# Experts' first rows and second rows gathered in separate phases, the second rows token by token and summed over partitions by TensorE, with five dense passes instead of four

## The chip, the cores and the metric

The kernel runs on one core of one Trainium2 chip. The metric is the device time of one execution in microseconds (us); lower is better. TensorE is called PE here, VectorE DVE, ScalarE ACT, GpSimd POOL and SyncE SP, as in the profile.

## The reference

Two layers over 512 tokens of 1,024 features, in float32. Each layer mixes tokens (attention and a recurrence), normalises, and then lets each token use 128 of 16,384 "experts", each of which is one row `u` and one row `v`:

```python
# one layer, cut to what matters
m = x @ w_in                                   # q, k, v, recurrent branch, gates
y = sigmoid(ga) * (DiffAttention(m) @ w_br_attn) + sigmoid(gr) * (RGLRU(m) @ w_br_lru)
x = layer_norm(ALPHA * x + y @ w_out)
# experts: 8 heads choose 16 rows each from the scores of two sets of 128 keys
e, g = choose(x @ peer_wq, subkeys)            # (token, 128) indices and weights
act = gelu(einsum('cd,ced->ce', x, u[e]))      # dot of the token with its 128 u rows
ffn = einsum('ce,ced->cd', g * act, v[e])      # weighted sum of its 128 v rows
x = layer_norm(ALPHA * x + ffn)
```

## The kernel before, in words

Tokens are cut into four blocks of 128, one token per partition. A *dense pass* (`mixer`, `route`, `route_late`) takes a pair of blocks of one layer from the projections to the choice of experts. It reads 96 chunks of weights, 512 KB each, through SP's DMA queue; `proj_T` and `proj_N` multiply them. There are four passes. The first one, with which nothing else can run, uses split operands (`Acts`): each float32 value is the sum of two float32r parts, and each product is made of three float32r products. The others use plain float32.

The *experts* (`experts`) of a block are 128 gathers, one per chosen expert rank j. A gather is one indirect DMA from POOL (line 730): for each of the 128 tokens, the 8 KB row of its j-th expert, `u` and `v` side by side, 1 MB in all. DVE multiplies the first half of the tile by the tokens and sums it (line 733: the dot); for every two gathers three small DVE operations and two small ACT operations turn the dots into weights; then the second half is added to the result either by DVE (line 703, into `acc`) or by PE (line 709), which multiplies it by a diagonal matrix that ACT makes out of the weights (line 707) and accumulates over the gathers in PSUM (`pv`). There are 1,024 gathers and 8 gather buffers.

The order of the work is written by `run`: gathers are a stream, and each dense pass is spread over a span of gathers by the table `PLAN`; a scheduler then fixes the order on each engine. A block's gathers begin when its first experts are chosen, so nothing is gathered until the first pass is nearly through.

Of the kernel before, what the change touches and what calls it, by code (L numbers as in the profile page):

```python
# [52 lines left out]
PLAN = (  # L53
# [4 lines left out]
)  # L58
V_ALONE = 0.5
MAXN = P * max(len(p[1]) for p in PLAN)  # L60
C_CHUNK = 1.75  # weight of 8 products of [128, 128] by [128, 128] in the issue order
HGS = {True: (1, 1, 2, 2, 2), False: (2, 2, 2, 2)}  # heads whose experts are chosen together


def weave(a, b, pace=1.0):
# [12 lines left out]
class Acts:  # L78
# [3 lines left out]
    def __init__(self, plain=None, hi=None, lo=None):  # L82
        self.plain = plain
        self.hi, self.lo = hi, lo
        self.split = plain is None


class Decoder:
    def __init__(self, ctx, tc, x, wpk, gpk, spk, cpk, lnv, lqk, uv, out):
        self.tc, self.nc = tc, tc.nc  # L90
        self.x, self.wpk, self.gpk, self.spk = x, wpk, gpk, spk
        self.cpk, self.lnv, self.lqk, self.uv, self.out = cpk, lnv, lqk, uv, out
# [6 lines left out]
        self.gp = pool("gather", 8)  # L99
        self.pp = pool("peer", 2)  # L100
        PS = dict(space=bass.MemoryType.PSUM)
        self.ps_mm = pool("ps_mm", 2, **PS)
        self.ps_s = pool("ps_s", 1, **PS)
        self.ps_t = pool("ps_t", 1, **PS)
        self.ps_v = pool("ps_v", 1, **PS)

    # ---------------------------------------------------------------- set-up
    def setup(self):
# [3 lines left out]
        # base bias: B[p, m] = (m - 384) - p where that is <= 0, else a large negative  # L112
# [10 lines left out]
        self.lnrows = cp.tile([16, 512], F32, name="lnrows")  # L123
        self.junk_a = cp.tile([P, P], BF16, name="junk_a")
# [3 lines left out]
        # tokens in two halves; the second's room serves the first dense part before  # L128
# [4 lines left out]
        self.e = [cp.tile([P, P], I32, name=f"e{b}") for b in range(NB)]  # L133
        self.g = [cp.tile([P, P], F32, name=f"g{b}") for b in range(NB)]
# [8 lines left out]
    def room(self, tag, dtype=F32, pool=None):  # L143
        """[128, 8, 256] for activations, in one of a few places."""
# [3 lines left out]
    def layer_consts(self, l):  # L148
# [18 lines left out]
        # softplus(-lambda) = log1p(exp(-|lambda|)) + max(-lambda, 0)  # L167
# [26 lines left out]
    # ---------------------------------------------------------------- helpers  # L194
# [5 lines left out]
    def split_weight(self, hi, lo, l, ch):  # L200
        """A chunk's weights in float32r parts whose sum they are."""
        raw = self.wp.tile([P, D], F32, name="raw", tag="w")
        self.nc.sync.dma_start(raw, self.wpk[l, ch])
        self.nc.scalar.copy(hi, raw)  # L204
        self.nc.vector.tensor_tensor(lo, raw, hi.bitcast(F32), ALU.subtract)  # L205

    def proj_T(self, l, ch, act, n, ps=None):
        """[chunk columns, tokens] of (tokens) @ w."""
        if ps is None:
            ps = self.ps_mm.tile([P, 512], F32, name="ps_mm", tag="mm")  # L210
        if act.split:
            t = self.gp.tile([P, 2, D], F32R, name="wsp", tag="uv")
            self.split_weight(t[:, 0], t[:, 1], l, ch)
            hi, lo = (t[:, i].rearrange("p (k c) -> p k c", k=KC) for i in range(2))
            passes = ((hi, act.hi), (hi, act.lo), (lo, act.hi))
        else:
            passes = ((self.weight(l, ch), act.plain),)
        steps = [(w[:, kc, :], x[:, kc, :n]) for w, x in passes for kc in range(KC)]
        for i, (w, x) in enumerate(steps):
            self.nc.tensor.matmul(ps[:, :n], w, x, start=i == 0, stop=i == len(steps) - 1)  # L220
        return ps

    def proj_N(self, l, ch, act, blocks):
# [458 lines left out]
    def experts(self, l, b, G=2):  # L682
# [60 lines left out]
        for _ in prev:  # L743
            pass
# [92 lines left out]
```

## Time and profile before

| | |
|---|---|
| time, median of 3 runs (lowest to highest) | 3567.16 us (3563.05 to 3572.27) |
| profiled execution, span | 3564.2 us |
| busy: PE, DVE, ACT, POOL | 83%, 81%, 30%, 35% |
| moved by DMA | 1290.77 MB, 362 GB/s over the span |

The span is the time from the first to the last instruction of the one execution that was profiled; no other time of that execution is shown. It lies 3 us under the median of the timed runs and within their range, so a sum made against the span can be read as a time of the runs, give or take those 3 us. The shares are averages over stages with different limits.

### The profile page before, as it was taken

Reading aid. Unit: us, or ns where it says so; the run is one execution under the profiler, and the core shown is the slowest. Engines: PE = TensorE matmul, PEld = TensorE weight load, DVE = VectorE, ACT = ScalarE, POOL = GpSimd, SP = SyncE. Lnnn points to the kernel's source line nnn. Section 1 sums busy time; section 2 is a strip of 40 time slices with the busy share of each in tenths; the row PEclk is TensorE's granted clock in tenths of the full one; section 3 lists DMA queues with packets and bytes.
Section 4 is the critical chain, followed back from the end, with each engine's and each line's share of the span. In section 5 each row is a group of like instructions: output and inputs, shape, how many; then the busy total and the mean of one; then the engine's idle time right before and its main releaser. Section 6 shows DMA issues by size and latency. Waiting matters only on the chain.

```text
span 3564.2 us, 41600 instructions
## 1 busy us (share of the span) xinstructions
PE 2963.9 (83%) x11804; PEld 1907.9 (54%) x11804; DVE 2883.3 (81%) x9658; ACT 1085.1 (30%) x3174; POOL 1264.4 (35%) x1033
## 2 busy tenths in 40 slices
PE   8996878999999689999998689999898676655555
PEld 7995635677756346777654256677755222211111
DVE  7765799998768987777778977798778977788887
ACT  7842213442122234421222134432122121112111
POOL 0001234344332333333332443333333344456553
PEclk9997999999999889999999799999999889877777
DMA  6454889999999899999999899999999899999997
GB/s 200 159 167 178 299 326 384 390 411 416 418 385 366 341 362 403 390 375 387 395 396 365 296 409 395 371 409 418 418 382 349 298 394 421 421 421 407 422 421 318
DMA packets 219141, 1290.77 MB, mean 362 GB/s; under 512 B 24592, under 2 KB 37136, under 8 KB 87840
## 3 DMA queue, kind: packets, MB, share of 16 engines
q0 software_dynamic: 147456, 1073.81, 75.1%
q1 hardware_dynamic: 71456, 214.30, 16.1%
q8 instruction: 96, 1.57, 0.2%
q14 instruction: 133, 1.09, 0.1%
HBM read 1285.92 MB, written 2.10 MB: 361 GB/s over the span
## 4 chain that ended last, share of the span: by engine, by line
PE 35%; DVE 29%; DMA 20%; issue 8%; POOL 4%; ACT 4%; POOLq 0%; SPq 0%; DVEq 0%; ACTq 0%
DMA uvt<-uv_dram,e 20%; PE ps_mm L220 14%; PE pv L709 12%; DVE uvt L733 10%; DVE junk_d L660 5%; PE ps_mm L242 4%; POOL uvt L730 4%; DVE acc L703 3%; DVE si L627 1%; DVE sv L625 1%; PE ps_ln L297 1%; PE s L348 1%; PE pg L451 1%; PE ps_qk L220 1%; DVE ca L645 1%
## 5 line engine op out<-in xcount | busy, mean ns | idle before, releaser
L730 POOL DMA_INDIRECT uvt<-uv_dram,e x1024 | 1261.8, 1232 | 2268.7 <-DVE acc L703 598.8
L709 PE MATMUL pv<-uvt,dg 128*128 128x512 f32 x2588 | 1394.3, 680 | 483.3 <-ACT dg L707 481.9
L733 DVE SCALAR_TENSOR_TENSOR uvt<-uvt,xn 128x1024 f32<-128x1024 f32 x1024 | 1243.9, 1220 | 180.6 <-DMA uvt<-uv_dram,e 179.5
L709 PEld LDWEIGHTS pv<-uvt,dg 128*128 128x128 f32 x2588 | 521.0, 213 | 1206.7 <-ACT dg L707 703.2
L220 PE MATMUL ps_mm<-room_xT,w 128*128 128x256 f32 x3072 | 717.2, 382 | 3.4 <-ACT room_xT L252 2.9
L220 PEld LDWEIGHTS ps_mm<-room_xT,w 128*128 128x128 f32 x3072 | 576.5, 191 | 140.3 <-issue 58.6
L738 ACT ACTIVATE q<-dots 128x2 f32<-128x2 f32 x512 | 103.7, 203 | 1284.0 <-DVE uvt L733 1234.7
L703 DVE SCALAR_TENSOR_TENSOR acc<-uvt,w,acc 128x1024 f32<-128x1024 f32 x377 | 483.2, 1282 | 8.1
L707 ACT ACTIVATE dg<-ident,w 128x128 f32<-128x128 f32 x647 | 241.9, 397 | 184.7 <-DVE w L696 117.5
L660 DVE SCALAR_TENSOR_TENSOR junk_d<-iota,pf,ca 128x54 bf16<-128x54 f32 x1024 | 215.9, 268 | 0.4
L693 ACT ACTIVATE q<-q 128x2 f32<-128x2 f32 x512 | 103.7, 202 | 212.9 <-DVE q L691 204.3
L691 DVE SCALAR_TENSOR_TENSOR q<-q,dots 128x2 f32<-128x2 f32 x512 | 81.3, 159 | 103.2 <-ACT q L738 72.6
L696 DVE SCALAR_TENSOR_TENSOR w<-q,w 128x2 f32<-128x2 f32 x512 | 80.5, 157 | 88.0 <-ACT q L693 86.4
L205 DVE TENSOR_TENSOR wsp<-raw,wsp 128x1024 fp32r<-128x1024 f32 x96 | 116.2, 1221 | 18.3 <-ACT wsp L204 18.0
L220 PE MATMUL ps_mm<-room_xT,wsp 128*128 128x256 f32 x768 | 114.9, 292 | 0.5 <-ACT wsp L204 0.5
L204 ACT CAST wsp<-raw 128x1024 fp32r<-128x1024 f32 x96 | 98.7, 1047 | 20.1 <-issue 6.0
L220 PEld LDWEIGHTS ps_mm<-room_xT,wsp 128*128 128x128 f32 x768 | 102.0, 196 | 4.7 <-issue 2.4
L242 PE MATMUL ps_mm<-w,room_m 128*128 128x128 f32 x768 | 92.1, 282 | 6.9 <-DVE room_m L508 6.9
L242 PEld LDWEIGHTS ps_mm<-w,room_m 128*128 128x128 f32 x768 | 91.3, 198 | 12.0 <-DVE room_m L508 7.5
L242 PEld LDWEIGHTS ps_mm<-w,room_xT 128*128 128x128 f32 x768 | 92.6, 195 | 9.4 <-issue 7.7
L625 DVE MAX8 sv<-sc 128x8 f32<-128x128 f32 x128 | 36.5, 289 | 73.2 <-ACT sc L590 64.6
L242 PE MATMUL ps_mm<-w,room_xT 128*128 128x128 f32 x768 | 94.6, 278 | 0.0
(193 smaller groups left out, 3030.9 us busy)
## 6 DMA issues: line engine op xcount, KB each, us to landing
w<-wpk_dram SPq DMA_DIRECT2D x288, 512.0 KB
raw<-wpk_dram SPq DMA_DIRECT2D x96, 512.0 KB
uvt<-uv_dram,e POOLq DMA_INDIRECT x1024
gw<-gpk_dram SPq DMA_DIRECT2D x32, 128.0 KB
sk<-spk_dram SPq DMA_DIRECT2D x64, 64.0 KB
xn<-x_dram SPq DMA_DIRECT2D x4, 512.0 KB
out_dram<-xn SPq DMA_DIRECT2D x8, 256.0 KB
lq<-lqk_dram SPq DMA_DIRECT2D x2, 128.0 KB
```

The lines of the kernel that those rows point to most:

```text
L204: self.nc.scalar.copy(hi, raw)
L205: self.nc.vector.tensor_tensor(lo, raw, hi.bitcast(F32), ALU.subtract)
L220: self.nc.tensor.matmul(ps[:, :n], w, x, start=i == 0, stop=i == len(steps) - 1)
L242: self.nc.tensor.matmul(out[:, i], x(slice(i * P, (i + 1) * P)), w, start=j == 0, stop=j == len(steps) - 1)
L660: nc.vector.scalar_tensor_tensor(out=self.junk_d[:, k % 4, :NCAND], in0=self.iota, scalar=pf[:, h, k : k + 1], in1=ca[:, 1, h], op0=ALU.is ...
L693: nc.scalar.activation(q, q, AF.Tanh, scale=C_GELU)
L703: nc.vector.scalar_tensor_tensor(out=acc, in0=t[:, D:], scalar=w[:, i : i + 1], in1=acc, op0=ALU.mult, op1=ALU.add)
L707: nc.scalar.activation(dg, self.ident, AF.Copy, scale=w[:, i : i + 1])
L709: nc.tensor.matmul(pv[:, half], dg, t[:, D + half * 512 : D + (half + 1) * 512], start=not used[1], stop=j == P - 2)
L730: nc.gpsimd.indirect_dma_start(out=t, out_offset=None, in_=self.uv, in_offset=bass.IndirectOffsetOnAxis(ap=e[:, j : j + 1], axis=0))
L733: nc.vector.scalar_tensor_tensor(out=t[:, :D], in0=t[:, :D], scalar=1.0, in1=x, op0=ALU.mult, op1=ALU.mult, accum_out=dots[:, i : i + 1])
L738: nc.scalar.activation(q, dots, AF.Square, scale=A_GELU)
```

## The change

The table of rows is cut in two, `u` and `v`. A block's experts become two phases. `phase_u` gathers the 128 first rows per rank as before (line 625), but only their 4 KB; the dots read the tokens from a copy in PSUM (`xps`). When all 128 are there, the weights are made for the whole block at once and transposed by PE. `phase_v` gathers the second rows by token: one gather takes the 128 rows of one token, one per partition, with the transposed indices `eT`. PE then sums over the partitions: the weights of the token are the one non-zero column of a strip of 32 columns (`ring`), and four tokens that lie in different quarters of the partitions write four strips of 32 partitions of `pv` (line 681). DVE adds no more rows, ACT makes no more diagonals. There are 2,048 gathers of 512 KB and 13 gather buffers of half the size.

`STREAM` is the order of the phases: u of the first block; u of the second beside v of the first, alternately; v of the second; and so on for each pair. The dense passes are five: blocks 0 and 1 of the first layer have one each, with products of 128 columns, and all passes use plain float32. PSUM is now four banks used by turns for all dense work (`bank`), two for `xps` and two for `pv`.

```diff
+STREAM = [s for l in range(2) for h in (0, 2) for s in (
+    (("u", l, h),), (("u", l, h + 1), ("v", l, h)), (("v", l, h + 1),))]
 PLAN = (
-    (0, [0, 1], 0, 0, 32, 64, (0.5, 0.0, 0.0)),
-    (0, [2, 3], 60, 205, 245, 360, (0.7, 0.0, 0.25)),
-    (1, [0, 1], 258, 430, 485, 600, (0.7, 0.0, 0.25)),
-    (1, [2, 3], 516, 690, 740, 860, (0.7, 0.0, 0.25)),
+    (0, [0], 0, 0, 70, 70),
+    (0, [1], 6, 104, 126, 126),
+    (0, [2, 3], 130, 385, 500, 636),
+    (1, [0, 1], 516, 860, 1010, 1148),
+    (1, [2, 3], 1028, 1400, 1520, 1660),
 )
...
-        self.gp = pool("gather", 8)
+        self.gp = pool("gather", 13)
...
-        self.ps_mm = pool("ps_mm", 2, **PS)
-        self.ps_s = pool("ps_s", 1, **PS)
-        self.ps_t = pool("ps_t", 1, **PS)
+        self.ps_mm = pool("ps_mm", 4, **PS)
+        self.ps_x = pool("ps_x", 1, **PS)
         self.ps_v = pool("ps_v", 1, **PS)
...
+        if h0 + HG == H:
+            ps = self.bank("ps_e")
+            nc.tensor.transpose(ps[:, :P], self.eF, self.ident)
+            nc.vector.tensor_copy(self.eT[b], ps[:, :P])
...
+    def phase_u(self, l, b):
...
+        for j in range(P):
...
+            if j == 0:
+                x = self.ps_x.tile([P, D], F32, name="xps", tag="xps")
+                nc.scalar.copy(x, self.xn[b])
+            t = self.row(self.u, self.e[b][:, j : j + 1])
+            nc.vector.scalar_tensor_tensor(out=t, in0=t, scalar=1.0, in1=x, op0=ALU.mult,
+                                           op1=ALU.mult, accum_out=dots[:, j : j + 1])
...
+        ps = self.bank("ps_w")
+        nc.tensor.transpose(ps[:, :P], dots, self.ident)
...
+    def phase_v(self, l, b):
...
+        for r in range(32):
...
+            for g in range(4):
+                t = 32 * g + r
+                ts.append(self.row(self.v, self.eT[b][:, t : t + 1]))
...
+            for half in range(2):
+                for g in range(4):
+                    o = 32 * (8 * g + k) + 31 - r
+                    nc.tensor.matmul(pv[32 * g : 32 * g + 32, half], ring[:, o : o + 32],
+                                     ts[g][:, half * 512 : (half + 1) * 512], start=r == 0,
+                                     stop=r == 31)
```

Three places of the engines' orders. First POOL, whose rows are the gathers (`e_108` to `e_111` are the indices of blocks 0 to 3; of the change `e_106`, `e_107` those of blocks 0 and 1, and `eT_110` the transposed ones of block 0), behind the last constant. Before:

```order
L121 IOTA iota 128x54
L730 DMA uvt<-uv_dram,e_108 128x2048 x128
L730 DMA uvt<-uv_dram,e_109 128x2048 x128
L730 DMA uvt<-uv_dram,e_110 128x2048 x128
L730 DMA uvt<-uv_dram,e_111 128x2048 x128
```

And of the change:

```order
L625 DMA row<-u_dram,e_106 128x1024 x128
L625 DMA row<-u_dram,e_107 128x1024
L625 DMA row<-v_dram,eT_110 128x1024
L625 DMA row<-u_dram,e_107 128x1024
L625 DMA row<-v_dram,eT_110 128x1024
```

No second row is gathered before the first gather of block 1's first rows is issued. Next DVE in the change, from dot 128, the last of block 0 (line 641 is the dot; lines 305 to 310 are the softmax of block 1's attention, 387 to 436 its recurrence, 646 and 649 make the weights of block 0):

```order
L641 SCALAR_TENSOR_TENSOR row,dots<-row,xps 128x1024
L305 SCALAR_TENSOR_TENSOR pr<-base,ps_s 128x256 x2
L428 SCALAR_TENSOR_TENSOR thx<-thx,xc 128x128
L309 TENSOR_REDUCE at_st<-pr 128x2
L422 SCALAR_TENSOR_TENSOR mu<-mu,tl 128x128
L310 TENSOR_SCALAR at_st<-at_st 128x2
L387 COPY xr<-hist 128x3
L646 SCALAR_TENSOR_TENSOR q<-q,dots 128x128
L649 TENSOR_TENSOR dots<-dots,g_118 128x128
L430 SCALAR_TENSOR_TENSOR mu<-thx,mu 128x128
```

In this place 386 DVE instructions, the rest of block 1's dense pass with its output projection (line 488) and its layer norm and a part of its choice of experts, stand before dot 129, and no dot among them. Last PE, in the middle of a dense pass. Before (line 709 adds second rows, 128 columns of weights by 512; the others are dense products):

```order
L242 MATMUL ps_mm<-w,room_xT 128x128 x16
L348 MATMUL s_11621<-kT_104,qT 128x128 x2
L709 MATMUL pv<-uvt,dg 128x512 x4
L374 MATMUL pt<-ident,pr 128x128 x2
L220 MATMUL ps_mm<-room_xT,w 128x256 x2
```

And of the change, where the second rows of block 0 begin (line 681; the first size is the 32 partitions of the strip):

```order
L653 MATMUL ps_w<-ident,dots 128x128
L230 MATMUL ps_xt<-ident,xn_4987 128x128 x8
L681 MATMUL pv<-row,ring_114 32x512
L209 MATMUL ps_mm<-room_xT,w 128x256 x16
L681 MATMUL pv<-row,ring_114 32x512 x7
L209 MATMUL ps_mm<-room_xT,w 128x256 x8
L402 MATMUL pg<-xc,gw 128x256 x2
```

Sums of second rows now come eight at a time (four tokens by two halves) and wait for the four gathers of their tokens.

## Rows read from the trace of the kernel before

**Rows 1.** Page, parts 1 and 2: span, engines, DMA in 40 slices.

```profile
span 3564.2 us, 41600 instructions
...
PE 2963.9 (83%) x11804; PEld 1907.9 (54%) x11804; DVE 2883.3 (81%) x9658; ACT 1085.1 (30%) x3174; POOL 1264.4 (35%) x1033
...
DMA  6454889999999899999999899999999899999997
GB/s 200 159 167 178 299 326 384 390 411 416 418 385 366 341 362 403 390 375 387 395 396 365 296 409 395 371 409 418 418 382 349 298 394 421 421 421 407 422 421 318
```

**Rows 2.** Page, part 3: DMA queues; packets, MB, share of 16 engines.

```profile
q0 software_dynamic: 147456, 1073.81, 75.1%
q1 hardware_dynamic: 71456, 214.30, 16.1%
```

**Rows 3.** Windows: length, then PE, PEld, DVE, ACT, POOL, PEclk, DMA share, GB/s.

```profile
0.00:319.00 319.00, 287.64 (x2208) 271.93 (x2208) 213.26 (x545) 196.95 (x386) 2.57 (x9) 0.97 0.48 156
319.00:550.00 231.00, 171.92 (x673) 103.93 (x674) 198.44 (x1186) 57.84 (x185) 69.69 (x62) 0.91 0.86 322
...
1000.00:1300.00 300.00, 248.21 (x755) 140.59 (x754) 257.71 (x1403) 75.91 (x255) 98.95 (x88) 0.90 0.90 357
1300.00:1800.00 500.00, 479.72 (x2069) 343.93 (x2068) 368.99 (x901) 164.90 (x502) 176.73 (x146) 0.96 0.98 391
...
1900.00:2100.00 200.00, 143.95 (x319) 65.40 (x318) 178.07 (x935) 43.19 (x145) 79.51 (x64) 0.85 0.90 342
...
2700.00:2900.00 200.00, 142.59 (x334) 66.16 (x333) 179.07 (x1001) 38.38 (x144) 70.12 (x64) 0.88 0.88 328
2900.00:3530.00 630.00, 381.87 (x590) 128.42 (x589) 502.35 (x999) 116.35 (x405) 331.88 (x251) 0.80 1.01 419
```

**Rows 4.** DMA from 3250 to 3500 us: gathers of 8 KB rows alone.

```profile
DMA packets 14461, 105.36 MB, mean 421 GB/s; under 512 B 1602, under 2 KB 1602, under 8 KB 1602
```

**Rows 5.** DMA from 9 to 14 us: weights in rows of 4 KB alone.

```profile
DMA packets 607, 2.03 MB, mean 406 GB/s; under 512 B 70, under 2 KB 126, under 8 KB 607
```

**Rows 6.** Groups of DVE by form: line, count, busy us, mean ns, idle.

```profile
L733 DVE SCALAR_TENSOR_TENSOR uvt<-uvt,xn 128x1024 f32<-128x1024 f32 x1024 | 1243.9, 1220 | 180.6 <-DMA uvt<-uv_dram,e 179.5 <-issue 0.3
L703 DVE SCALAR_TENSOR_TENSOR acc<-uvt,w,acc 128x1024 f32<-128x1024 f32 x377 | 483.2, 1282 | 8.1
L660 DVE SCALAR_TENSOR_TENSOR junk_d<-iota,pf,ca 128x54 bf16<-128x54 f32 x1024 | 215.9, 268 | 0.4
...
L746 DVE SCALAR_TENSOR_TENSOR xn<-acc,pv 128x1024 f32<-128x1024 f32 x8 | 9.8, 1220 | 3.7 <-PE pv L709 3.4
```

**Rows 7.** Line 730, POOL's gathers: shortest, median, longest ns; first and last start.

```profile
L730 POOL DMA_INDIRECT uvt<-uv_dram,e x1024: 935/942/3133, 319.9 to 3532.5; - x171
```

**Rows 8.** Timeline of POOL near the end: start, length, line, idle before.

```profile
3253.83 1.94 POOL L730 DMA_INDIRECT uvt<-uv_dram,e  x1 [0.30 <-issue]
...
3274.20 0.94 POOL L730 DMA_INDIRECT uvt<-uv_dram,e  x1 [0.30 <-issue]
3275.44 0.94 POOL L730 DMA_INDIRECT uvt<-uv_dram,e  x1 [0.30 <-issue]
```

**Rows 9.** Timeline of DVE at the same place, two dots in a row.

```profile
3254.87 1.22 DVE L733 SCALAR_TENSOR_TENSOR uvt<-uvt,xn 128x1024 f32<-128x1024 f32 x1
...
3256.01 1.22 DVE L733 SCALAR_TENSOR_TENSOR uvt<-uvt,xn 128x1024 f32<-128x1024 f32 x1
```

**Rows 10.** Timeline of PE in the second pass.

```profile
813.49 1.88 PE L709 MATMUL pv<-uvt,dg 128*128 128x512 f32 x4
815.30 1.14 PE L348 MATMUL s<-kT,qT 64*128 64x256 f32 x8
...
828.43 3.72 PE L220 MATMUL ps_mm<-room_yr,w 128*128 128x256 f32 x16
```

**Rows 11.** Groups of PE by form: dense products of 128 columns.

```profile
L242 PE MATMUL ps_mm<-w,room_m 128*128 128x128 f32 x768 | 92.1, 282 | 6.9 <-DVE room_m L508 6.9
```

More of the change, by code (lines that the diff above doesn't have):

```diff
@@ L133, in setup @@
         self.e = [cp.tile([P, P], I32, name=f"e{b}") for b in range(NB)]
+        self.eT = [cp.tile([P, P], I32, name=f"eT{b}") for b in range(NB)]
+        self.w = {}
+        self.ring = [cp.tile([P, 32 * (RING + 1)], F32, name=f"ring{i}") for i in range(2)]
+        for r in self.ring:
+            nc.gpsimd.memset(r, 0.0)
         self.g = [cp.tile([P, P], F32, name=f"g{b}") for b in range(NB)]
@@ L198, in weight @@
         return w
[L200 to L220, printed above, removed]
-        return ps
@@ L264, in transpose_x, with bank, proj_T, proj_N @@
-    def transpose_x(self, act, i, b):
+    def bank(self, name):
+        return self.ps_mm.tile([P, 512], F32, name=name, tag="mm")
+    def proj_T(self, l, ch, x, n):
+        ps = self.bank("ps_mm")
+        w = self.weight(l, ch)
+        for kc in range(KC):
+            self.nc.tensor.matmul(ps[:, :n], w[:, kc, :], x[:, kc, :n], start=kc == 0,
+                                  stop=kc == KC - 1)
+        return ps
+    def proj_N(self, l, ch, x, blocks):
+        ps = self.bank("ps_mm")
+        w = self.weight(l, ch)
+        out = ps.rearrange("p (b c) -> p b c", c=P)
+        for i in range(len(blocks)):
+            for kc in range(KC):
+                self.nc.tensor.matmul(out[:, i], x[:, kc, i * P : (i + 1) * P], w[:, kc, :],
+                                      start=kc == 0, stop=kc == KC - 1)
+        return out[:, : len(blocks)]
@@ L271, in transpose_x, with layer_norm @@
                                     self.xn[b][:, kc * P : (kc + 1) * P], self.ident)
-            self.keep(act, (slice(None), slice(half * 4, half * 4 + 4), slice(i * P, (i + 1) * P)),
-                      ps.rearrange("p (k t) -> p k t", k=4))
-    def layer_norm(self, l, which, rows, eps, junk):
+            nc.scalar.copy(x[:, half * 4 : half * 4 + 4, i * P : (i + 1) * P],
+                           ps.rearrange("p (k t) -> p k t", k=4))
+    def layer_norm(self, l, which, rows, eps):
         nc, t2 = self.nc, self.t2
@@ L322, in project @@
         def project(h):
[L324 to L325 removed]
+            pk = self.proj_T(l, CH_K + h, x, n)
             k0 = t0 % (2 * P)
@@ new lines, in phase_v @@
+    def phase_v(self, l, b):
+        nc, pp = self.nc, self.pp
+        yield ("weights", l, b)
+        pv = self.ps_v.tile([P, 2, 512], F32, name="pv", tag="pv")
+        w = self.w[l, b].rearrange("p (g r) -> p g r", g=4)
+        x = self.xn[b]
+        for r in range(32):
+            ring, k = self.ring[r // 8 % 2], r % 8
+            if k == 0:
+                nc.scalar.copy(
+                    ring[:, 31 : 31 + 32 * RING].rearrange("p (k c) -> p k c", c=32)[:, :, 0]
+                    .rearrange("p (g k) -> p g k", g=4), w[:, :, r : r + 8])
+            ts = []
+            for g in range(4):
+                t = 32 * g + r
+                ts.append(self.row(self.v, self.eT[b][:, t : t + 1]))
+                if g < 3:
+                    yield 1
+            for half in range(2):
+                for g in range(4):
[3 more added lines that the diff above has]
+                                     stop=r == 31)
+            yield 1
@@ L756, in run @@
         self.done = set()
-        self.share = 0.5
         def gathers():
-            for l in range(DEPTH):
-                for b in range(NB):
-                    yield from self.experts(l, b)
+            for place in STREAM:
+                parts = [getattr(self, f"phase_{k}")(l, b) for k, l, b in place]
+                while parts:
+                    for p in list(parts):
+                        c = next(p, None)
+                        while isinstance(c, tuple):
+                            yield c
+                            c = next(p, None)
+                        if c is None:
+                            parts.remove(p)
+                        else:
+                            yield c
         def dense():
-            for l, blocks, j0, j1, j2, j3, shares in PLAN:
+            for l, blocks, j0, j1, j2, j3 in PLAN:
                 if l:
```

290 lines of the change are left out of this document (94 added, 196 removed).

## The prediction

> **What bounds the kernel now.** I read the page first. Over the span PE is busy 83%, DVE 81%, the DMA carries 362 GB/s [rows 1]; three resources at four fifths each say only that stages differ, so I went to the slices and then to windows of time. In the last 630 us the DMA share is 1.01 and the rate 419 GB/s, with DVE at 80% and PE at 61% [rows 3]: there the transfers alone set the time. Gathers with nothing beside them reach 421 GB/s [rows 4], so a gather of 1.05 MB costs 2.49 us and the 1,024 gathers, 1,073.81 MB [rows 2], cost 2,551 us of the 3,564. The remaining megabytes, at the 406 GB/s of weights alone [rows 5], make it some 3,080 us. About 480 us are lost, and the windows say where [rows 3]: 0 to 319 us moves 156 GB/s, because no gather exists until 319.9 us [rows 7], which loses some 196 us; 319 to 550 moves 322 (53); 1000 to 1300, 1900 to 2100 and 2700 to 2900 move 357, 342 and 328, and DVE is busy 86 to 90% in them (44, 36 and 43); 1300 to 1800 moves 391 with PE busy 96% (32). The rest is spread over the other stretches and the 32 us behind the last gather. So the kernel is bound by bytes, less a late start and stretches in which DVE or PE cannot keep up.
>
> **What the change does to the bytes.** The gathered bytes stay. The extra dense pass reads 96 more chunks of 512 KB and some constants, 52 MB. Together 1,074 + 214 + 52 + 3 for instructions = 1,343 MB. All rows are now 4 KB. The only rows of 4 KB seen alone are weights, at 406 GB/s [rows 5]; so I price everything at 406: a gather of 512 KB is 1.291 us, all bytes are 3,308 us. Of the 230 us by which that exceeds 3,080, about 94 come from gathers at 406 instead of 421 and 129 from the fifth pass. For the bounds: 421 if the size of a row costs nothing; and 373, which is the share of the weights' queue over the whole run, 214.30 MB in 16.1% of 3,564 us [rows 2].
>
> The Trainium skill ("DMA: Bandwidth & Descriptors", the anatomy of one DMA) gives 2.0 us plus bytes at 436 GB/s for one such DMA, with half efficiency near 860 KB, which speaks against halving a gather: 3.2 us alone by it, an estimate, and 2,048 of them one after the other would be over 6,500 us. The weights, 512 KB each and up to five in flight, ran at 406 GB/s [rows 5], so the fixed part lies beside other transfers here, and I charge nothing for it; eight gathers stay in flight as before.
>
> **POOL** issues twice as often. An undisturbed issue takes 0.94 us and 0.30 until the next [rows 8]: 1.24 us, 4% under the 1.291 of the transfer. 2,048 issues are 2,540 us, under the bytes, but without slack within a phase. Some issues take 1.94 us [rows 8], beside DVE work; the median of all is 942 ns, the longest 3,133 [rows 7]. If the dots' new operand in PSUM leaves more issues undisturbed, nothing is lost; if a tenth are long, 0.1 x 1.0 x 1,920 would be 190 us of which a queue of eight hides most. I take this into the 2.5% below.
>
> **DVE** loses the 377 additions into `acc`, 483 us [rows 6], some 1,536 small operations on weights (about 240 us) and the splits of the first pass (about 116). It keeps 1,024 dots and the choice of experts, whose largest part is 216 us [rows 6]. The dots follow each other every 1.14 us though each is listed with 1.22 [rows 9]; with tokens from PSUM the nearest row is line 746, also 1,220 ns [rows 6], so I leave 1.145 (bounds 1.14 and 1.28, the form with `acc`). That is 147 us per block against 165 us of its gathers. Where u and v alternate, DVE has one dot for two gathers; DVE stops being a bound except in the four phases of u alone.
>
> **PE** now sums all second rows. A product of 128 columns of weights by 512 is two records, four records take 1.88 us [rows 10], about 0.43 us each, 0.86 a product. The change has 256 of them per block, in strips of 32 columns. One after the other: 220 us a block; four side by side: 55. No row shows strips of columns; the nearest shows strips of 64 rows: eight records of 256 columns in 1.14 us [rows 10], where eight in a row at 3.72 us for 16 [rows 10] would take 1.86, so strips do run beside each other. I take 55 and keep 220. The Trainium skill ("TensorE: Matmul & The Clock Gate", Part 3) has three column strips at 2.38 times one after the other; four in proportion would make it about 69 us a block, an estimate, and the sum would be the same, since 69 is still under 165.
>
> Dense products of 128 columns take 0.24 us (92.1 us busy over 384 products, two records each) [rows 11], against 0.47 for 256 columns [rows 10]: two passes of one block cost PE what one pass of two does. PE's dense total in the change is about 1,590 us, of which 388 stand before the first second row.
>
> **The sum by stages.** (A) To the first gather: the first pass has 80 chunks of 8 products at 0.24 us, 154, and some 20 of attention and recurrence; a pass alone ran PE at 90% (288 of 319 us) [rows 3], so 193, plus 10 of first loads and about 12 for the first choice: 215 us, against 319.9. (B) The 128 first rows of block 0 beside half of the second pass: 165 + 50 chunks at 1.291 = 230. Then the rest of that pass, 386 DVE instructions with no dot among them, and behind them the next dot; POOL can run ahead only 13 buffers, and second rows wait their turn behind block 1's first. Half a pass of PE is 97, at 90% 108, and 27 for norm and choice: 135. So B is 365, of which some 70 us leave the DMA without work. (C) Everything else: 1,920 gathers at 1.291 = 2,479 and three passes of 52 MB at 406 = 389, together 2,870. How much is lost on top? The best stretch loses 0.5% (419 of 421), the one with PE at 96% loses 6% (391 of about 416) [rows 3]. PE has 2,964 us of work now [rows 1] and about 2,030 in the change (1,590 + 8 x 55), DVE 2,883 [rows 1] and about 2,050, so most of C should look like the best stretch, and the phases of u alone beside a choice of experts like the worse: 2.5%, 72 us. (D) Behind the last gather: the last strips, sum and norm, 22 us in place of 32. 215 + 365 + 2,942 + 22 = **3,545 us**, 19 under the profiled span of 3,564 and 22 under the median of 3,567. The gain of some 105 us at the start and of the losses behind DVE is nearly eaten by the fifth pass and the smaller rows.
>
> **Rivals.** *Strips one after the other.* If PE runs the four strips in sequence, a block's second rows cost it 220 us. A phase of v alone (165 of gathers plus a few weights, 165 to 186) then takes 220 plus its dense 0 to 62: +96, +81, +89, +55. The alternating ones with dense work of 339, 219 and 225 us become 559, 439 and 445 against 445, 394 and 394: +114, +45, +51. Sum +531, **4,075 us**. It decides from about 165 us a block on. For it: each strip needs its own weights loaded, and no column strips are in the trace; against it, the row strips [rows 10]. The Trainium skill's page "TensorE: Matmul & The Clock Gate" (Part 3), above, speaks against it as well.
> *Rows of 4 KB at 373 GB/s.* C becomes 2,870 x 406 / 373 = 3,124, with the other terms **3,726** (3,800 with the 2.5%). For it: the queue's share [rows 2]; against it that this share holds waits and short packets.
> *Dense chain as the bound.* All dense work and the weights share four PSUM banks in turn, and C loses 6% everywhere as from 1300 to 1800 us [rows 3]: 580 + 2,870 x 1.06 + 22 = **3,644**.
> *Saturated throughout.* C loses only 0.5%: **3,487**. If a row's size costs nothing (421), C is 2,768 with 2.5% on top 2,837, in all **3,439**.
>
> **Chances.** My forecast with its spread of 3,480 to 3,620: 0.50. Saturated or 421: 0.14. Dense chain: 0.13. 373: 0.08. Serial strips: 0.15. A measurement of this kernel tells about 0.3% from no change, 3,556 to 3,578. The forecast's own part is 0.27 below that, 0.11 within, 0.12 above; with the rivals 0.41 faster, 0.11 the same, 0.48 slower. The serial strips stay outside the range: 3,440 to 3,760.
>
> **What would show it.** First gather near 215 us; a hole of some 70 us with low DMA between dot 128 and the first second rows; then a DMA share near 1 at about 406 GB/s wherever gathers run, and windows of rows of 4 KB alone that say 421, 406 or less; the four strips of line 681 starting within nanoseconds of each other, or one behind the other with v phases of over 200 us; POOL at 0.94 us with 0.3 between; DVE well under 70% of the span. I am wrong if gathers wait for a buffer that PE holds, if POOL's issues are mostly long, or if the late passes hold block 2's or the second layer's experts back so that gathers stop as they do in B.

## The result

| | before | changed |
|---|---|---|
| time, median (lowest to highest) | 3569.05 us (3563.05 to 3572.27) | 4095.28 us (4089.62 to 4106.70) |
| profiled execution, span | 3564.2 us | 4091.9 us |

The ratio is 1.1487, 95% interval 1.1464 to 1.1509: 526 us slower, outside the range of 3,440 to 3,760. The runs were made on several chips: the kernel before takes 3,563 to 3,569 us on all of them, but the changed kernel takes 4,095 us on one and 3,847 us on another (e13). Two chips gave the longer times (runs e1 to e8) and two the shorter ones (e9 to e18); below they are called the first kind and the second kind. Times of kernels with 4 KB rows are compared on one kind, or the text says where not.

The page of the changed kernel answers to [rows 1] and [rows 2]: the span, the engines, DMA in 40 slices, the queues.

```profile
span 4091.9 us, 44532 instructions
...
PE 2996.9 (73%) x14136; PEld 1731.1 (42%) x14136; DVE 2183.3 (53%) x7925; ACT 646.9 (16%) x1638; POOL 1935.3 (47%) x2059
...
DMA  7689777889788799999998799899998699999998
GB/s 256 234 326 339 283 254 284 329 321 355 271 293 292 281 341 386 374 338 363 351 359 302 280 366 384 328 358 336 379 353 307 209 361 385 362 370 365 371 352 333
...
q0 software_dynamic: 294912, 1073.87, 70.3%
q1 hardware_dynamic: 88736, 266.74, 18.4%
```

DVE fell to 53%, POOL doubled its issues and is at 47%, the megabytes are as forecast (1,343.45 in all). But no slice reaches 406 GB/s, not even the last ones, in which no dense work is left. Its costly groups (line, names, count, busy us, mean ns, idle):

```profile
L625 POOL DMA_INDIRECT row<-u_dram,e x1024 | 969.4, 947 | 1139.8 <-DVE eF L604 394.6
L625 POOL DMA_INDIRECT row<-v_dram,eT x1024 | 961.5, 939 | 999.4 <-PE pv L681 447.1
L641 DVE SCALAR_TENSOR_TENSOR row<-row,xps 128x1024 f32<-128x1024 f32 x1024 | 1224.8, 1215 | 386.3 <-DMA row<-u_dram,e 187.5
L681 PE MATMUL pv<-row,ring 128*32 128x512 f32 x4096 | 1153.5, 685 | 276.1 <-DMA row<-v_dram,eT 233.5
```

POOL's issue is 0.94 us, as in [rows 8], and the dots with tokens from PSUM cost what they did [rows 6]. The second rows' gathers wait 447 us for line 681, the sums on PE. These are busy 1,153 us: 144 a block, where the sum of the prediction had 55. POOL's starts give the phases, between gathers 0, 128, 384, 512 and so on; beside each stands what its megabytes take at 406 GB/s. The two right-hand columns are e13 and e15, below, on another chip.

| phase (us) | bytes at 406 | changed | again (e13) | without sums (e15) |
|---|---|---|---|---|
| to the first gather | | 207 | 209 | 208 |
| layer 0: u of block 0 | 300 | 404 | 391 | 390 |
| u of 1 and v of 0 | 446 | 586 | 533 | 432 |
| v of 1 | 190 | 262 | 242 | 222 |
| u of 2 | 200 | 218 | 200 | 209 |
| u of 3 and v of 2 | 409 | 471 | 460 | 410 |
| v of 3 | 183 | 246 | 228 | 197 |
| layer 1: u of 0 | 198 | 214 | 203 | 203 |
| u of 1 and v of 0 | 408 | 470 | 446 | 411 |
| v of 1 | 181 | 266 | 246 | 199 |
| u of 2 | 167 | 180 | 166 | 165 |
| u of 3 and v of 2 | 331 | 364 | 334 | 333 |
| v of 3 | 165 | 186 | 171 | 164 |

Two things are in it. Behind the first phase, the six in which sums meet dense work (the three mixed ones with a dense pass, and the v phases behind them) lose most: 62 to 140 us each over their bytes. And on the first kind of chip even the last three, with no dense work, run 8 to 13% over theirs.

### The profile page after: what moved, and what is told of

Its sections match the earlier page's. It is cut to its first block, busy times and chain, and to the rows that moved or that the text cites. A ratio compares the mean times of both kernels' runs of the same rounds, so it can differ in the third digit from the quotient of the medians.

```text
span 4091.9 us, 44532 instructions
## 1 busy us (share of the span) xinstructions
PE 2996.9 (73%) x14136; PEld 1731.1 (42%) x14136; DVE 2183.3 (53%) x7925; ACT 646.9 (16%) x1638; POOL 1935.3 (47%) x2059
## 2 busy tenths in 40 slices
DMA packets 383882, 1343.45 MB, mean 328 GB/s; under 512 B 42896, under 2 KB 58512, under 8 KB 383648
## 4 chain that ended last, share of the span: by engine, by line
PE 48%; DVE 18%; issue 15%; DMA 7%; POOL 5%; ACT 3%; another core or an unknown queue 3%; POOLq 0%; ACTq 0%; SPq 0%; DVEq 0%
PE ps_mm L209 25%; PE pv L681 11%; DVE row L641 9%; PE ps_mm L220 5%; POOL row L625 5%; DMA row<-v_dram,eT 4%; DVE junk_d L594 3%; DMA row<-u_dram,e 2%; PE po L332 1%; PE ps_s L303 1%; PE ps_sc L518 1%; PE ps_ln L257 1%; PE pg L402 1%; PE pt L326 1%
## 5 line engine op out<-in xcount | busy, mean ns | idle before, releaser
L625 POOL DMA_INDIRECT row<-u_dram,e x1024 | 969.4, 947 | 1139.8 <-DVE eF L604 394.6
L625 POOL DMA_INDIRECT row<-v_dram,eT x1024 | 961.5, 939 | 999.4 <-PE pv L681 447.1
L641 DVE SCALAR_TENSOR_TENSOR row<-row,xps 128x1024 f32<-128x1024 f32 x1024 | 1224.8, 1215 | 386.3 <-DMA row<-u_dram,e 187.5
L681 PE MATMUL pv<-row,ring 128*32 128x512 f32 x4096 | 1153.5, 685 | 276.1 <-DMA row<-v_dram,eT 233.5
L209 PE MATMUL ps_mm<-room_xT,w 128*128 128x256 f32 (+1 forms) x5120 | 1040.5, 356 | 15.4 <-issue 7.0
L209 PEld LDWEIGHTS ps_mm<-room_xT,w 128*128 128x128 f32 x5120 | 844.9, 202 | 253.0 <-issue 151.5
L681 PEld LDWEIGHTS pv<-row,ring 128*32 128x32 f32 x4096 | 191.7, 116 | 1026.4 <-DMA row<-v_dram,eT 645.5
L594 DVE SCALAR_TENSOR_TENSOR junk_d<-iota,pf,ca 128x54 bf16<-128x54 f32 x1024 | 214.3, 271 | 43.8 <-DVE junk_d L594 37.8
L209 PE MATMUL ps_mm<-room_yr,w 128*128 128x256 f32 (+1 forms) x640 | 130.4, 358 | 0.0
L209 PE MATMUL ps_mm<-room_ya,w 128*128 128x256 f32 (+1 forms) x640 | 123.0, 341 | 0.0
L209 PEld LDWEIGHTS ps_mm<-room_yr,w 128*128 128x128 f32 x640 | 108.3, 202 | 24.8 <-issue 12.6
```

The costliest lines, as they stand in the source:

```text
L209: self.nc.tensor.matmul(ps[:, :n], w[:, kc, :], x[:, kc, :n], start=kc == 0, stop=kc == KC - 1)
L594: nc.vector.scalar_tensor_tensor(out=self.junk_d[:, k % 4, :NCAND], in0=self.iota, scalar=pf[:, h, k : k + 1], in1=ca[:, 1, h], op0=ALU.is ...
L625: self.nc.gpsimd.indirect_dma_start(out=t, out_offset=None, in_=table, in_offset=bass.IndirectOffsetOnAxis(ap=index, axis=0))
L641: nc.vector.scalar_tensor_tensor(out=t, in0=t, scalar=1.0, in1=x, op0=ALU.mult, op1=ALU.mult, accum_out=dots[:, j : j + 1])
L681: nc.tensor.matmul(pv[32 * g : 32 * g + 32, half], ring[:, o : o + 32], ts[g][:, half * 512 : (half + 1) * 512], start=r == 0, stop=r == 31)
```

## The experiments

Theory 1: the strips of PE cost the time (first as the prediction's rival, strips in sequence). Theory 2: rows of 4 KB move slower. Theory 3: PE waits inside a group of four gathers. Theory 4: gathers of 4 KB rows leave no slack. Theories 3 and 4 came with the runs.

**e1_lab** leaves out all but one dense pass and makes gathers of seven kinds in a row:

```diff
+        for j in range(P):
+            self.touch(U(j))                    # A, G; B with V, F with pairs of rows
+        for j in range(P):
+            self.dot(U(j), j)                   # C
+        for r in range(32):
+            self.strips([V(32 * g + r) for g in range(4)], r)   # D; E: C and D by turns
```

> A laboratory kernel: the first dense pass of block 0 alone, then 128 gathers each of seven kinds one behind the other, with 10 buffers: (A) first rows, each only touched by ACT (one column read); (B) second rows by token, only touched; (C) first rows with their dots; (D) second rows with the strips of PE; (E) both kinds by turns, with dots and strips, 256 gathers; (F) pairs of neighbouring rows, 8 KB each, touched; (G) as A. Everything else of the computation is left out. Theory 1, the strips are what costs: A, B and G run at the rate of POOL's issues, 1.24 us each, 159 us and 410 to 422 GB/s, and D alone falls behind, over 200 us. Theory 2, random rows of 4 KB cost DMA rate whatever is done with them: A, B, C, D and G all take some 180 us, 360 to 373 GB/s, E 365 us, and F 319 us at 421 GB/s.

Measured, A to G without their first ten gathers (bytes of the packets between POOL's starts): 361 (its second half 410), 407, 329, 360, 368, 422 and 409 GB/s. DMA from 320 to 396 us, in A:

```profile
DMA packets 8548, 31.13 MB, mean 410 GB/s; under 512 B 952, under 2 KB 952, under 8 KB 8546
```

So neither theory held as it stood: 4 KB rows do reach the 406 of [rows 5] while nothing but a touch follows, and the rate fell with dots (C) as well as with strips (D). How it fell is seen in C (timeline; then 40 slices of DMA from 622 to 628 us):

```profile
618.55 1.22 DVE L634 SCALAR_TENSOR_TENSOR row<-row,xps 128x1024 f32<-128x1024 f32 x1 [1.31 <-DVE row L634]
618.81 0.94 POOL L625 DMA_INDIRECT row<-u_dram,e  x1 [1.86 <-DVE row L634]
619.96 0.08 DVE L634 DVE_READ_ACCUMULATOR row<-row,xps 128x1 f32 x1 [0.19 <-issue]
621.35 1.22 DVE L634 SCALAR_TENSOR_TENSOR row<-row,xps 128x1024 f32<-128x1024 f32 x1 [1.31 <-DVE row L634]
621.61 0.94 POOL L625 DMA_INDIRECT row<-u_dram,e  x1 [1.86 <-DVE row L634]
```

```profile
DMA  9642210097386388999962000009960575899996
GB/s 410 273 164 109 82 55 27 0 164 82 55 191 137 137 328 328 437 410 437 437 246 109 0 0 0 0 0 218 164 82 0 137 218 246 355 410 437 437 437 246
```

Dot and issue go in step, one gather every 2.80 us, though DVE needs 1.22 and POOL 1.24. The transfers come in bursts that start slowly, reach 437 GB/s and stop. But the transfers aren't what is waited for: by 620 us DMA had moved 41,608 packets of the gathers' queue, which at 144 a gather is 289 of the 290 that POOL had issued. Dot and issue both wait for the dot before (`<-DVE row L634`). Its last part ends at 620.04, and the next dot, released by its semaphore (the signal by which one instruction tells the next that it is done), starts at 621.35, 1.31 us later. The same place in the same kernel on a chip of the second kind (e16, below):

```profile
613.10 0.08 DVE L634 DVE_READ_ACCUMULATOR row<-row,xps 128x1 f32 x1
613.23 1.22 DVE L634 SCALAR_TENSOR_TENSOR row<-row,xps 128x1024 f32<-128x1024 f32 x1
```

There the next dot starts 0.05 us behind, and POOL issues a gather every 1.28 us.

**e2_nosum** leaves out 30 of a block's 32 groups of sums:

```diff
-            for half in range(2):
+            if r in (0, 31):
+                ...
+            else:
+                for g in range(4):
+                    nc.scalar.copy(self.mark, ts[g][:, :1])
```

> The changed kernel without 30 of each block's 32 groups of strips: ACT reads one column of each gathered tile in their place, so the sums of second rows are mostly left out. Theory 1 (the strips cost the 531 us that the rival gave them): about 3,560 us. Theory 2 (the DMA rate of 4 KB rows): the phases of second rows still run at about 366 GB/s, and only the stalls in which PE or POOL wait on one another go, at most some 210 us: 3,880 to 4,090.

Measured 3,753.96 us, ratio 1.0541 (1.0519 to 1.0562), between both: on this kind of chip the sums cost some 340 us, and 190 us over the kernel before remain without them.

**e3_serial** writes all strips of groups 1 to 30 to the same partitions:

```diff
+                    q = 32 * g if r in (0, 31) else 0
-                    nc.tensor.matmul(pv[32 * g : 32 * g + 32, half], ring[:, o : o + 32],
+                    nc.tensor.matmul(pv[q : q + 32, half], ring[:, o : o + 32],
```

> The changed kernel with the strips of groups 1 to 30 all written to the same 32 partitions, so that they can't lie side by side; the sums are those of four tokens together. Theory 1, strips already run one after the other: no change, 4,095 us. If they lie side by side, as busy PE of line 681 (144 us a block where four in sequence would take 220) suggests, PE gets some 76 us more per block, and where it holds the end that is up to 600 us: 4,300 to 4,700. Theory 2 alone with PE hidden: under 4,300.

Measured 4,588.05 us, ratio 1.2868 (1.2841 to 1.2894), and line 682, the sums, in its groups of PE:

```profile
L682 PE MATMUL pv<-row,ring 128*32 128x512 f32 x4096 | 1804.4, 618 | 94.2 <-DMA row<-v_dram,eT 81.3 <-issue 11.9 <-ACT wT L655 0.6
```

225 us a block, the 220 of the rival. So the strips of the change do lie side by side, and the rival that came within 20 us of the result is false.

**e4_before_4k** and, on another chip, **e17_before_4k_again**: the kernel before with two gathers of 4 KB a rank.

```diff
+                for part, table in enumerate((self.u, self.v)):
+                    nc.gpsimd.indirect_dma_start(
+                        out=t[:, part * D : (part + 1) * D], out_offset=None, in_=table,
```

> The kernel before with the table cut in two and two gathers of 4 KB rows for each rank into the two halves of the same tile, nothing else changed. Theory 2 (366 GB/s for gathers of 4 KB rows against 421): 1,074 MB take 2,934 us in place of 2,551, so up to 380 us more, 3,850 to 3,950. Theory 1 (rows of 4 KB at 406): 94 us more, some 3,660, if POOL's 2,048 issues of 1.24 us stay hidden.

> The same kernel as e4_before_4k (3,804 us). There POOL took 1.26 us an issue behind DVE's work and 0.30 to the next, 3.1 us for the two gathers of a rank against 2.49 of transfer, and the last 870 us ran at 330 to 343 GB/s. That belongs to POOL and stays on any chip; if it is all, 3,780 to 3,810 again. If the slow transfers of 4 KB rows had a part in it, on a chip without them: 3,660 to 3,740.

Measured 3,804.38 (ratio 1.0661, 1.0611 to 1.0710) and 3,757.16 us (1.0534, 1.0515 to 1.0553), each between its two ranges. In the second, POOL from 3100 to 3650 us:

```profile
L731 POOL DMA_INDIRECT uvt<-u_dram,e x174 | 226.7, 1303 | 53.1 <-issue 35.4 <-DVE w L696 9.8 <-DMA uvt<-u_dram,e 5.5
L731 POOL DMA_INDIRECT uvt<-v_dram,e x174 | 217.7, 1251 | 53.0 <-issue 51.5 <-DMA uvt<-u_dram,e 1.5
```

Beside DVE's work with both operands in SBUF an issue takes 1.25 to 1.30 us on average (0.93 at least, 1.99 at most), and 0.30 follow: 3.16 us a rank where two gathers take 2.56 at 410 GB/s. There POOL is the bound, at some 330 GB/s; the two chips differ by 47 us. In the change, whose dots read the tokens from PSUM, the issue stays at 0.94.

**e5_lag** and, on another chip, **e18_lag_again** issue a group's products after the next four gathers:

```diff
+            if late is not None:
+                self.strips(pv, *late)
+            late = (ts, ring, k, r)
```

> The changed kernel with the eight products of four tokens issued one group later (after the next four gathers of second rows), nothing else. Theory 3: PE comes to a group before its four gathers have landed, so that products meant to lie side by side run one by one and dense work waits behind them (busy PE of line 681 is 144 us a block, the group at 1131 us took 1.92, which is 61 a block). Then the busy time of line 681 falls to about 500 to 700 us from 1,153, and the time to some 3,850 to 4,000 us. Rival: the four tiles more that are held leave too few of the 13 buffers for gathers under way; then line 681 gets shorter and the time does not, 4,090 to 4,250.

> The same kernel as e5_lag (sums issued one group later). On a chip without the slow transfers the changed kernel took 3,847 us. If PE's waiting inside a group is a part of what the sums cost there: 3,700 to 3,800. If not: 3,820 to 3,850. On a chip with them: 4,067 again.

Measured 4,067.40 (ratio 1.1414, 1.1395 to 1.1433) and 3,820.79 us (1.0711, 1.0689 to 1.0733): 28 and 26 us less than the change on a chip of the same kind (the last two phases, worked out as in the table, take 364 and 187 us in the first, 333 and 171 in the second). The sums stay at 1,151 and 1,112 us, far from the 500 to 700 of theory 3. PE's order is fixed by a scheduler, so moving the code moves the products only in part: the move brought 0.7%, and what PE's waiting inside a group costs in all isn't shown.

**e6_buf9**: `pool("gather", 9)` in place of 13.

> The changed kernel with 9 gather buffers in place of 13. If buffers held by groups that wait for PE set the gathers' pace (POOL waited 528 us for line 681), it is slower by 100 to 300 us: 4,200 to 4,400. If the pace is set elsewhere (rate of 4 KB rows, PE's work): under 4,130.

Measured 4,105.87 us, ratio 1.1499 (1.1478 to 1.1520): under the 4,130 that was expected if the pace is set elsewhere. Four buffers less cost 11 us.

**e7_four** makes blocks 0 and 1 one pass, `(0, [0, 1], 0, 0, 64, 126)`.

> The changed kernel with the first two blocks of layer 0 in one dense pass again, in plain float32: four passes. By the bytes: 129 us less to move, a start some 110 us later, and no dense work beside the first rows of block 0, whose phase (404 us) becomes some 170 to 230: 3,960 to 4,030 us. If the stages behind are bound by PE and not by bytes, the gain is only that of the first two stages.

Measured 4,117.35 us, ratio 1.1546 (1.1523 to 1.1569): missed. The first gather comes at 412 us in place of 207, and what the bytes save goes there: going back to four passes gains nothing here.

**e8_before_five** gives the kernel before the five passes:

```diff
-    (0, [0, 1], 0, 0, 32, 64, (0.5, 0.0, 0.0)),
-    (0, [2, 3], 60, 205, 245, 360, (0.7, 0.0, 0.25)),
+    (0, [0], 0, 0, 32, 32, (0.5, 0.0, 0.0)),
+    (0, [1], 3, 100, 124, 124, (0.7, 0.0, 0.25)),
+    (0, [2, 3], 126, 240, 270, 370, (0.7, 0.0, 0.25)),
```

> The kernel before with five passes: blocks 0 and 1 of layer 0 one after the other in plain float32, the rest as it was, with gathers of 8 KB rows. The first gather comes near 208 us in place of 320, and 52 MB more are read, 129 us at 406 GB/s. If both count in full: 3,563 - 112 + 129 = 3,580 us. If the second pass lies beside the 128 gathers of block 0 at a full DMA (319 + 129 us) and the loss between 319 and 550 us goes away too: 3,520 to 3,550. If its dense work holds block 1's experts back as in the changed kernel: over 3,600.

Measured 3,632.09 us, ratio 1.0184 (1.0167 to 1.0201). The first gather starts at 203 us, but from 208 to 700 the DMA already runs at 400 to 402 GB/s, so the added megabytes count in full (129 us) and use up the head start (117). The other 50 us or so are lost in the two blocks behind: gathers 128 to 384 run at 363 and 341 GB/s where the kernel before has 393 and 379; why isn't shown. So in the kernel before five passes are a loss of 1.8%.

**e9_tiny** cuts the products of groups 1 to 30 to 16 columns (`n = 512 if r in (0, 31) else 16`).

> The changed kernel with the products of groups 1 to 30 cut to 16 of their 512 columns: PE still waits for every gather of second rows and frees its tile, but spends next to no time on it; most of each sum is left out. If the 341 us that the sums cost (4,095 against 3,754 without them) are PE's time, it comes near 3,754: 3,740 to 3,830. If they are PE waiting in its fixed order for gathers, with dense work behind, most of them stay: 3,980 to 4,100.

Measured 3,661.43 us, ratio 1.0273 (1.0257 to 1.0288), below both, which speaks for PE's time; but this ran on a chip of the second kind, so its distance is to e13 (3,847), not to 4,095.

**e10_plan_late** and **e14_plan_late_again**, on two chips, spread the dense passes:

```diff
-    (0, [2, 3], 130, 385, 500, 636),
-    (1, [0, 1], 516, 860, 1010, 1148),
-    (1, [2, 3], 1028, 1400, 1520, 1660),
+    (0, [2, 3], 130, 430, 511, 630),
+    (1, [0, 1], 516, 940, 1023, 1142),
+    (1, [2, 3], 1028, 1452, 1535, 1654),
```

> The changed kernel with the dense passes of blocks 2 and 3 and of the second layer spread over more gathers: their mixers end at gather 430, 940 and 1452 in place of 385, 860 and 1400, the choices of experts follow up to gathers 630, 1142 and 1654. If PE has too much to do where first and second rows alternate (85 to 90% busy there) and less in the phases of second rows alone, this evens it out: 3,980 to 4,060 us. If it only moves the late point to the next phase: 4,090 to 4,200.

> The same kernel as e10_plan_late. If the plan brought the 198 us: as far below after_again as then, ratio to it about 0.952. If the chip brought most of it: within 60 us of after_again.

Measured 3,897.59 (ratio 1.0933, 1.0914 to 1.0952) and 3,898.76 us (1.0927, 1.0903 to 1.0951). Beside 4,095 the first looked like a gain of 198 us; beside e13 on its own chip the plan is 52 us slower. The same time on both chips lets e9 be compared with e13 and e15.

**e11_before_share**: shares (0.7, 0.0, 0.0) in the kernel before.

> The kernel before with one number of its table changed: while the second block's experts are chosen, PE adds all second rows (share 0.0 in place of 0.25 for DVE). DVE is 86 to 90% busy in those stretches and PE about 72%; it loses some 25 of 100 gathers' additions at 1.28 us three times. If DVE is the bound there, up to 90 us less: 3,480 to 3,550. If not: 3,560 to 3,575.

Measured 3,599.76 us, ratio 1.0089 (1.0074 to 1.0104): missed, and 33 us the other way. The three stretches run at 359, 347 and 323 GB/s where the kernel before has 357, 342 and 328 [rows 3], so DVE's additions aren't the bound there; where the 33 us go isn't shown.

**e12_lab2**, gathers of seven other kinds (dots over 512 columns: `in0=t[:, :512]`), on the chip of e9 and e10.

> The laboratory kernel again, 128 gathers each, 10 buffers: (A) 4 KB rows touched; (H) 4 KB rows with dots over 512 of the 1,024 columns; (C) with whole dots; (K) second rows with the strips of one half, 4 products of 8; (D) with all strips; (M) 8 KB rows with one dot each; (N) 8 KB rows with two dots each. Theory 4: a gather of 4 KB rows leaves its consumer and POOL no slack (1.28 us of transfer, 1.24 of issue, 1.14 to 1.27 of a dot), and what is lost once is not made up; then H and K run near 410 GB/s, C and D at 330 to 370, M at 421, N (2.44 us of DVE for 2.49 of transfer) dips too. Rival: rows of 4 KB dip whenever they are read in full or in half; then H and K run at 360 as well.

Measured, in the order of the expectation and as in e1: 389 (with a disturbed start), 409, 405, 407, 409, 422, 422 GB/s. C and D, at 329 and 360 in e1, ran freely: neither theory 4 nor its rival. The same instructions behave differently on different chips; the next four runs share one chip.

**e13_after_again** (the change itself), **e15_nosum_again** (e2) and **e16_lab_again** (e1), with e14:

> The changed kernel unchanged. If the state of the DMA belongs to the chip: 4,095 us where the last phase runs at 360 GB/s (186 us), and about 3,950 to 4,020 where it runs at 405 (166 us). If it belongs to the program's own history: 4,095 us and 186 us again on any chip.

> The same kernel as e2_nosum (30 of 32 groups of the sums left out). On a chip whose last phase runs at 405 GB/s: 3,640 to 3,700, as e9_tiny; on one at 360 GB/s: 3,754 again. Its distance to after_again is what the sums cost.

> The same kernel as e1_lab. If the chip decides: dots (C), strips (D) and both (E) all near 408 GB/s on a chip where after_again's last phase is at 405, and 329 to 370 on one where it is at 360. If the program decides: 329 to 370 on any chip.

Measured: 3,846.88 us (ratio 1.0782, 1.0761 to 1.0803), 3,561.26 us (0.9984, 0.9974 to 0.9995), and 1,711.30 us for the laboratory (one run) where e1 took 1,818.93. The chip decides, and by more than expected: the first two lie under their ranges. The GB/s of the laboratory's page, first e1_lab, then e16_lab_again:

```profile
GB/s 248 238 193 293 271 317 311 409 410 409 410 409 375 286 287 388 360 361 355 368 358 382 359 378 370 370 359 371 367 424 422 422 422 422 421 422 411 410 407 329
```

```profile
GB/s 250 236 189 293 236 383 357 410 409 409 410 410 410 410 409 396 409 409 394 409 409 410 409 409 408 404 409 402 417 423 422 422 422 422 422 421 409 409 408 346
```

The 14th to 28th slices are dots and strips: 286 to 388 on one chip, 394 to 410 on the other; the 8 KB rows behind them are 422 on both. On this chip the sums cost 3,846.88 - 3,561.26 = 286 us. Six phases hold 285 of it by the table. Windows of e13 (length, PE, PEld, DVE, ACT, POOL, PEclk, DMA share, GB/s):

```profile
599.70:1132.30 532.60, 459.55 (x2563) 342.89 (x2562) 305.12 (x980) 131.26 (x312) 242.40 (x256) 0.92 0.91 340
1132.30:1374.50 242.20, 215.70 (x825) 76.91 (x823) 133.44 (x1080) 22.78 (x71) 120.06 (x129) 0.92 0.87 316
...
1574.90:2034.90 460.00, 409.86 (x1790) 233.14 (x1791) 227.62 (x600) 64.99 (x169) 240.34 (x256) 0.92 0.96 360
2034.90:2263.30 228.40, 198.21 (x741) 63.14 (x738) 118.06 (x944) 17.28 (x55) 120.02 (x129) 0.94 0.88 325
...
2465.80:2911.60 445.80, 389.02 (x1873) 242.52 (x1872) 231.28 (x495) 71.69 (x173) 241.30 (x257) 0.92 0.97 371
2911.60:3157.60 246.00, 216.93 (x802) 75.58 (x800) 132.27 (x1070) 21.40 (x66) 119.92 (x129) 0.92 0.82 298
...
3323.90:3657.40 333.50, 197.75 (x499) 29.97 (x499) 164.17 (x270) 3.93 (x9) 239.70 (x256) 0.78 1.02 406
```

and the first, third and fifth of these phases in e15:

```profile
597.90:1029.40 431.50, 320.32 (x1622) 273.35 (x1621) 286.93 (x917) 135.88 (x416) 242.83 (x256) 0.85 0.99 392
...
1459.40:1869.00 409.60, 263.49 (x1311) 224.04 (x1311) 230.22 (x603) 83.48 (x289) 240.73 (x256) 0.80 1.02 406
...
2269.40:2680.10 410.70, 273.00 (x1396) 233.03 (x1394) 232.52 (x496) 88.42 (x293) 241.50 (x257) 0.81 1.02 404
```

In the six, PE is busy 86 to 89% and the DMA share is 0.82 to 0.97; without sums PE falls to 64 to 74% in the three shown, and the DMA rises to 0.99 to 1.02. In the last row of e13, first and second rows by turns with no dense work, the same sums cost nothing: 406 GB/s.

## Why the prediction was wrong

*What held.* The first gather (215 forecast, 207), the megabytes, POOL's issue, the dots from PSUM, DVE's share, the 22 us at the end (last gather at 4,074, 18 us). The stop ahead of block 1's first gather was foreseen (135 us, measured 158 in e13); phase B took 404 us, in e13 391, for 365. Without the sums and on a chip of the second kind, the rest of the design takes 3,561 us for the forecast 3,545, and not by luck: A to D are 208, 390, 2,943 and 20 us there (e15) for 215, 365, 2,942 and 22.

*Step 1 that failed, PE.* "I take 55": the sums were costed as if a block's 256 products always ran four at a time, and as hidden since 55 is under 165. Neither held. Of the page of e13, the sums and the second rows' gathers:

```profile
L681 PE MATMUL pv<-row,ring 128*32 128x512 f32 x4096 | 1136.9, 673 | 251.2 <-DMA row<-v_dram,eT 250.4
L625 POOL DMA_INDIRECT row<-v_dram,eT x1024 | 961.9, 939 | 846.7 <-PE pv L681 410.9
```

Timeline of PE in the changed kernel, then in e13:

```profile
1131.24 1.92 PE L681 MATMUL pv<-row,ring 128*32 128x512 f32 x16
```

```profile
2101.72 0.71 PE L518 MATMUL ps_sc<-sk,pqT 128*128 128x128 f32 x4
2102.27 0.60 PE L209 MATMUL ps_mm<-room_xT,w 128*128 128x256 f32 x2
2102.80 1.04 PE L681 MATMUL pv<-row,ring 128*32 128x512 f32 x2
2103.77 0.70 PE L209 MATMUL ps_mm<-room_xT,w 128*128 128x256 f32 x2
2104.40 1.05 PE L681 MATMUL pv<-row,ring 128*32 128x512 f32 x2
2105.38 1.99 PE L209 MATMUL ps_mm<-room_xT,w 128*128 128x256 f32 x8
```

A whole group, 16 records, takes 1.92 us: 61 a block, 3.7 times as fast as in sequence (225, e3). The Trainium skill ("TensorE: Matmul & The Clock Gate", Part 3) has 2.38 times for three strips; the trace agrees that strips run beside each other, and has 3.7 times for four. But one product alone, two records between dense ones, takes 1.05. So a block costs 142 us (1,137 over eight in e13). Of the six phases, line 681 alone (length, PE, PEld, PEclk, DMA share, GB/s):

```profile
599.70:1132.30 532.60, 84.59 (x498) 16.73 (x498) 0.92 0.91 340
1132.30:1374.50 242.20, 131.74 (x496) 22.73 (x496) 0.92 0.87 316
...
1574.90:2034.90 460.00, 156.61 (x497) 24.78 (x498) 0.92 0.96 360
2034.90:2263.30 228.40, 135.67 (x499) 23.00 (x496) 0.94 0.88 325
...
2465.80:2911.60 445.80, 125.11 (x495) 20.70 (x496) 0.92 0.97 371
2911.60:3157.60 246.00, 135.28 (x500) 22.88 (x498) 0.92 0.82 298
```

There the sums are busy 769 us and not 330, and dense work takes the other 1,120 where the prediction's figures give at most 969 (339, 219 and 225 in the mixed phases, up to 62 in each v phase). Their sum, 1,889 us, is 88% of the six phases' 2,155 and more than the 1,817 that their bytes take, and taking columns away from the products (e9) shortens them: PE is the bound there. By the prediction's figures PE had at most 1,299 us (330 and 969), well hidden; in its sum it held the sums against the transfers of the second rows alone. Its own sign of being wrong is in the trace: gathers wait for tiles that PE holds, 411 us in e13. Of the 286 us, about 186 are the columns (e13 against e9, across two chips that agree on e10 and e14). The other 100 (e9 against e15, the same two chips) stay with products of 16 columns. These still keep PE busy for 202 us in the six phases (38 in e15), and PE has to come to them in its order; no run parts the two. The later issue brought back 26 (e18).

*Step 2 that failed, the time of a gather on the first kind of chip.* "I price everything at 406" holds on the second kind (410 touched, 405 to 409 with dots or strips, e12 and e16). On the first kind the change took 248 us more (4,095 against 3,847), e2 193 (3,754 against 3,561), e5 247, the laboratory 108. Slower rows aren't the reason: 4 KB rows reach 410 there too when only touched (e1). What comes late there is the semaphore between two instructions, as in e1's 2.80 us a gather, and also where no gather takes part. The choice of experts, from the page of the changed kernel and from that of e13:

```profile
L594 DVE SCALAR_TENSOR_TENSOR junk_d<-iota,pf,ca 128x54 bf16<-128x54 f32 x1024 | 214.3, 271 | 43.8 <-DVE junk_d L594 37.8
```

```profile
L594 DVE SCALAR_TENSOR_TENSOR junk_d<-iota,pf,ca 128x54 bf16<-128x54 f32 x1024 | 208.4, 272 | 0.4
```

These 1,024 instructions read no gathered row and do the same work, but on the first kind DVE waits 37.8 us for one to tell the next that it is done; in the kernel before it doesn't (0.4 idle, line 660 in [rows 6]). Counted by the trace's semaphore times, waits that end only with a semaphore that came over 0.3 us behind its instruction's end: 142 on DVE (98 us), 50 on POOL (34) and 43 on ACT (32) in the changed kernel, none in e13, e15, e16 and e18, none in the kernel before. The prediction's sum has nothing for this, and the trace of the kernel before has no sign of it. How much of the 248 us it makes isn't shown. The rival of 373 GB/s forecast 181 us more, which is near the 193 of e2 by luck, since its reason, a lower rate of 4 KB rows, is refuted by the 410.

*The sum of it:* 3,545 forecast, 16 of other terms, 286 of sums on PE, 248 of the first kind of chip: 4,095. Taken the other way round it is 193 of the chip and 341 of the sums; the two add to each other's cost.

*Left open.* Why semaphores come late on some chips with 2,048 gathers of 4 KB rows, and not with 1,024 of 8 KB. One rival has no run: the traces of the first kind have lost many records of landings (the changed kernel's holds 16,639 of 32,768, that of e13 32,745), so the recording itself may have a part in the delay; no run here goes without it. No version beat the kernel before: with the sums nearly left out, on the better kind of chip, the change is equal to it within 0.3%.

## What to carry to other kernels

Ask of work that is moved to another engine not whether it is shorter than the transfers, but what it adds to that engine in just the stretch where it falls, at the price it has when it comes in pieces between other work. A rival's time that agrees with the result proves nothing: serial strips forecast 4,075, and the run that made them serial took 4,588. Gathers of half the size leave POOL (1.24 us an issue for 1.28 of transfer) no room to catch up. Before a gain is read from two runs, run the reference beside it on the same chip; and where transfers look slow, see first whether the next gather had been asked for.

## What the runs showed of the hardware

Gathers of 4 KB rows move 409 to 410 GB/s when only touched, against 422 for 8 KB (e1, e16). With a consumer of the whole row their rate was 329 to 368 on one chip (e1) and 405 to 409 on two others (e12, e16), while the kernel before, with 8 KB rows, timed the same within 0.2% on every chip. In the slow stretch of e1 a dot started 1.31 us after the one before it had ended, for which it waited; in e16 0.05 us. An indirect issue of 128 rows takes 0.94 us beside dots with an operand in PSUM (e13) and 1.25 to 1.30 on average beside DVE work from SBUF alone (e17). Four strips of 32 columns side by side take 1.92 us for 16 records of 512 columns, two records alone 1.05 (e13); written to the same partitions, a block's sums take 225 us (e3).
